# Gates of an mLSTM layer: column sums and the norm's spread inside blocks of products, and a new order of the row work on three engines

## The chip, the cores and the metric

The kernel runs on one core of a Trainium2 chip. Times are microseconds of device time for one execution. The core has TensorE (PE in the profile, with its weight loads as PEld), VectorE (DVE), ScalarE (ACT), GpSimd (POOL), and SyncE (SP), which here issues the DMAs. The number that counts is the median of several executions.

## The reference

One inference step of a decoder trunk with two layers. Layer 0 mixes tokens with a gated MLP, layer 1 with an mLSTM (a matrix memory with 8 heads); each layer is followed by a gated MLP with a causal convolution. There are 256 prompt tokens and a sample group of 8 sequences of 8 new tokens, 320 tokens in all, and the model width is 1024. All is fp32. The change lies at the start of the mLSTM layer. What is computed there, cut down:

```python
h = rmsnorm(x, g)                        # x * rsqrt(mean(x*x) + EPS) * g
p = h @ w_in                             # columns: q, k | v | o | i, f
qk, new_buf = causal_dwconv(p[..., :QK_B], conv_buf, conv_w, conv_b)   # 4 taps
qk = silu(qk)
ig = i_pre + b_i                         # 8 heads
lf = log_sigmoid(f_pre + b_f)
# per head, over the tokens (the prompt as one run, each sample sequence as one)
b = cumsum(lf)
m = max(b + m0, max over s <= t of (b_t - b_s + ig_s))        # running maximum
w_intra = exp(b_t - b_s + ig_s - m_t);  w_inter = exp(b_t + m0 - m_t)
g = exp(b_last - b + ig - m_last);      decay = exp(b_last + m0 - m_last)
```

So the gates need two running sums along the 320 tokens, one additive and one of maxima, in 8 rows (one for each head), and a handful of exponentials of them. `m` at the end of every sequence is an output.

## The kernel before, in words

**Layout.** Activations are kept transposed: features on the 128 partitions, the 320 tokens along the free axis. A product of an activation with a weight is done in *blocks*: one block makes 128 output features for all 320 tokens from the 1024 input features, in 8 steps `k` of 128.

**Three products for one.** To reach fp32 accuracy with a faster type, each operand is split into a high and a low half. For the activations these are `xh` and `xl`. A weight of a block arrives as `raw` (a DMA that SyncE issues, L152), ScalarE casts it to the high half `wh` (L179), and VectorE subtracts that from `raw` to make the low half `wl` (L180). A block is thus 24 products of 320 columns: for the mLSTM layer, `chunk` first does the 16 products that need `wh` (`xh` and `xl` for 8 steps) and then, in a second sweep, the 8 that need `wl`.

**Order.** The products and transposes of TensorE stay in the order of the program (`mm` and `tr` pin them). The other engines' instructions are put in order by a scheduler that has its own idea of when each will be ready; `tc.issue_after(x)` keeps what is made under it behind instruction x. Weights are ahead of their use: `take()` hands out the halves of the next block, issues the load of the fourth block ahead (L152), and issues the split of the next one (L179, L180). So a block's low half is made on VectorE during the block before it, and VectorE executes in its own fixed order: a low half that stands behind a waiting instruction comes late.

**The norm.** x is not normalised ahead of the products: the products are made of x times the norm's gain, and the factor for each token is multiplied into the results. `norm_cols` adds the squares over the features with three small products (`pc`, tokens on the partitions afterwards), VectorE scales the sums and adds EPS (`ms`, L294), ScalarE copies the sample group's 64 values to the other half of the partitions (L296), and GpSimd takes the power -1/2 (`rc`, L297). `norm_row(split=False)` turns these columns into a row that is the same on all partitions: three diagonal matrices `dg` made by VectorE (L307), one fp32 product of a matrix of ones with them (`pb`), and a copy by ScalarE (`rb`). Elsewhere in the kernel `norm_diag` and `norm_spread` do the same with the factors split into a high part (`rch`, `dg`) and a low part (`dgl`, made by ScalarE) and two products of the faster type.

**The gates** (`gates`, L716 to L810). First come 16 products `pg` for the gates' pre-activations, then the column sums (four small steps), then the blocks of head 0, in this order: q, first half of v, k, second half of v, first and second half of o. The text calls them the first to the sixth block. The spread `pb` stands between the first and the second. After the sixth, three transposes `pt` turn the finished rows `RS` into columns. The rows' work lies beside the blocks:

- `zi` is the pre-activation times `rb` plus the bias; ScalarE makes log-sigmoid from an Exp and a Ln (`az`, L760 and L761), with loads of its function tables (L759 is one) between functions of different tables, and a one-element Tanh (L762) brings the table that the convolutions need;
- VectorE scans (`b`), makes `a` and `aM`, scans for the maxima (`M`, L774), and then `m`, `wi` (two pieces, L781 and L782), the two pieces of `X`, and `g` (two pieces);
- ScalarE makes Exp of `wi`, `g` and `m`; the output `mo` and the rows `Xf` leave by DMA.

`qk_epi` (L812) is what follows a block of q or k: GpSimd copies three state columns in front of each sample sequence (`bpad<-bst`, L817), VectorE multiplies the block by `rb` into `bpad`, ScalarE starts the convolution (`bcv`, L824), VectorE adds three taps (L826), ScalarE takes a tanh (`bth`), VectorE makes `qs` by two products with it and the low half of q or k. `v_epi` only copies, on ScalarE. VectorE's order in this stage before is: q's epilogue as far as its inputs are there, the log-sigmoid rows, the scans, then k's taps and the low half of the sixth block.

The lines that the change touches:

## Time and profile before

| | us |
|---|---|
| median of 3 runs (lowest to highest) | 884.53 (884.48 to 884.72) |
| the profiled execution | 884.82 |
| its span in the profile | 883.1 |
| TensorE busy in it | 876.1 (99%) |
| VectorE busy | 672.4 (76%) |
| ScalarE busy | 514.3 (58%) |
| GpSimd busy | 109.5 (12%) |

The granted clock of TensorE in the profiled execution was 0.999 of the full one. The stage that the change touches runs from about 394 us to 418 us of the span.

How to read the rows that follow: a row of the timeline begins with the start and the time taken, in microseconds from the start of the span, then the engine, the line of the kernel, the operation, what it writes and reads by the program's names, its shape, and how many of the kind stand in a row (x3). A bracket at the end tells how long the engine was idle before and which instruction of another engine ended that. PE rows with several products give the time from the first one's start to the last one's end, and neighbouring rows overlap, because products are pipelined: the pace is read from start to start. A row of the chain that ended last has start, time taken, engine, tile and line.

### The profile page before, as it was taken

The page shows a single profiled execution, that of the slowest core. Times are in us where ns is not written, and L with a number is a line of the kernel's source. Part 1 is how long each engine was busy: PE and PEld are TensorE (multiplying, and loading weights), DVE is VectorE, ACT ScalarE, POOL GpSimd, SP SyncE. Part 2 cuts the span into 40 slices and gives each one's busy share as a digit, 9 for nine tenths or more (in the row PEclk, how much of TensorE's full clock was granted, in tenths as well). Part 3 has the DMA queues.
Part 4 walks back from the last instruction along what each step waited for, and adds up shares of the span by engine and source line. Part 5 has one row for each costly group of instructions (what it writes and reads, how often), then busy time and mean ns, then how long its engine had stood idle before and what let it go on. Part 6 is the DMA issues. An engine that isn't in the chain of part 4 may idle for free.

```text
span 883.1 us, 17016 instructions
## 1 busy us (share of the span) xinstructions
PE 876.1 (99%) x6421; PEld 859.1 (97%) x6421; DVE 672.4 (76%) x1288; ACT 514.3 (58%) x932; POOL 109.5 (12%) x287
## 2 busy tenths in 40 slices
PE   9999999999999999999999999999999999999997
PEld 7889999999999999999999999999999999999997
DVE  6866985678878865558999998878998788786443
ACT  6668553565555544447777776656766555554342
POOL 3200000020000000002433212203002000000000
PEclk9999999999999999999999999999999999999999
DMA  8653446644455455554747766665664444555551
GB/s 256 236 191 127 137 144 180 213 162 157 157 168 167 148 169 165 155 184 163 231 150 234 239 223 219 199 214 166 196 226 156 165 155 161 168 160 165 154 152 60
DMA packets 55238, 156.15 MB, mean 177 GB/s; under 512 B 7492, under 2 KB 13132, under 8 KB 55156
## 3 DMA queue, kind: packets, MB, share of 16 engines
q1 hardware_dynamic: 55156, 155.06, 55.4%
q8 instruction: 51, 0.84, 0.4%
q14 instruction: 31, 0.25, 0.1%
HBM read 143.05 MB, written 11.99 MB: 176 GB/s over the span
## 4 chain that ended last, share of the span: by engine, by line
PE 96%; DVE 2%; DMA 1%; ACT 0%; SPq 0%; issue 0%; POOL 0%; DVEq 0%
PE pm L75 83%; PE pv_a L75 6%; PE num L75 2%; PE pmix L75 1%; PE pcs L75 1%; PE psc L75 1%; PE pCp L75 1%; PE phn L78 1%; PE pv L78 1%; DMA raw<-in_a_wv 1%; PE pc L75 0%; PE pk L78 0%; DVE bcv L826 0%; DVE wl L180 0%; PE pg L75 0%; PE pb L75 0%
## 5 line engine op out<-in xcount | busy, mean ns | idle before, releaser
L180 DVE TENSOR_TENSOR wl<-raw,wh 128x1024 fp32r<-128x1024 f32 (+4 forms) x254 | 298.0, 1175 | 110.8 <-ACT wh L179 108.4
L179 ACT CAST wh<-raw 128x1024 fp32r<-128x1024 f32 (+4 forms) x254 | 255.5, 1006 | 209.0 <-PE pm L75 141.3
L75 PE MATMUL pm<-xh,wh 128*128 128x320 f32 x1216 | 356.6, 301 | 0.0
L75 PE MATMUL pm<-xl,wh 128*128 128x320 f32 x1216 | 354.5, 299 | 0.0
L75 PE MATMUL pm<-xh,wl 128*128 128x320 f32 x1216 | 308.9, 299 | 0.1
L75 PEld LDWEIGHTS pm<-xh,wh 128*128 128x128 f32 x1216 | 229.9, 189 | 0.3 <-ACT vTb L845 0.2
L75 PEld LDWEIGHTS pm<-xl,wh 128*128 128x128 f32 x1216 | 229.9, 189 | 0.2
L75 PEld LDWEIGHTS pm<-xh,wl 128*128 128x128 f32 x1216 | 211.9, 189 | 0.3 <-DVE wl L180 0.3
L75 PE MATMUL pm<-yh_f,wl 128*128 128x320 f32 x352 | 105.2, 299 | 0.0
L75 PE MATMUL pm<-yh_f,wh 128*128 128x320 f32 x352 | 105.2, 299 | 0.0
L75 PE MATMUL pm<-yl_f,wh 128*128 128x320 f32 x352 | 105.2, 299 | 0.0
L75 PEld LDWEIGHTS pm<-yh_f,wh 128*128 128x128 f32 x352 | 66.5, 189 | 0.0
L75 PEld LDWEIGHTS pm<-yl_f,wh 128*128 128x128 f32 x352 | 66.5, 189 | 0.0
L75 PEld LDWEIGHTS pm<-yh_f,wl 128*128 128x128 f32 x352 | 66.5, 189 | 0.0
L577 DVE SCALAR_TENSOR_TENSOR fcv<-fpad,vecs,fcv 128x336 f32<-128x336 f32 x88 | 49.5, 565 | 2.1 <-ACT fcv L575 0.7
L579 ACT ACTIVATE fgl<-fcv 128x256 f32<-128x256 f32 x44 | 18.3, 415 | 37.3 <-DVE fcv L577 37.3
L75 PE MATMUL pm<-yh_a,wl 128*128 128x320 f32 x128 | 38.4, 300 | 0.0
L75 PE MATMUL pm<-yh_a,wh 128*128 128x320 f32 x128 | 38.4, 300 | 0.0
L75 PE MATMUL pm<-yl_a,wh 128*128 128x320 f32 x128 | 38.3, 299 | 0.0
L75 PE MATMUL pm<-yhb,wh 128*128 128x320 f32 x128 | 35.9, 304 | 0.0
L75 PE MATMUL pm<-ylb,wh 128*128 128x320 f32 x128 | 35.5, 300 | 0.0
L345 DVE TENSOR_TENSOR xT<-pm,xT 128x320 f32<-128x320 f32 x39 | 18.9, 486 | 19.0 <-PE pm L75 19.0
(276 smaller groups left out, 1261.5 us busy)
## 6 DMA issues: line engine op xcount, KB each, us to landing
raw<-in_f_up SPq DMA_DIRECT2D x88, 512.0 KB, 3.3
raw<-in_b_win SPq DMA_DIRECT2D x48, 512.0 KB, 4.3
raw<-in_f_dn SPq DMA_DIRECT2D x32, 448.0 KB, 3.3
C<-in_C SPq DMA_DIRECT2D x32, 258.0 KB, 5.3
out_Cs<-C SPq DMA_DIRECT2D x32, 258.0 KB, 4.6
raw<-in_a_win SPq DMA_DIRECT2D x16, 512.0 KB, 3.3
raw<-in_a_wo SPq DMA_DIRECT2D x16, 512.0 KB, 5.2
raw<-in_f_dn SPq DMA_DIRECT2D x16, 512.0 KB, 3.5
```

The source lines that it names most:

```text
L75: self.pin(self.nc.tensor.matmul(out, lhsT, rhs, start=start, stop=stop, skip_group_check=skip))
L78: self.pin(self.nc.tensor.transpose(out, in_, ident))
L179: self.last_split = self.hold(nc.scalar.copy(wh[:, :kn, :], raw[:, :kn, :]))
L180: self.last_low = nc.vector.tensor_tensor(wl[:, :kn, :], raw[:, :kn, :], wh[:, :kn, :].bitcast(F32), op=SUB)
L345: self.nc.vector.tensor_tensor(x, ps[:, :T], x, op=ADD)
L577: nc.vector.scalar_tensor_tensor(cv, pd[:, i:i + NC], self.vec(w + i * KF), cv, op0=MULT, op1=ADD)
L579: nc.scalar.activation(gl[:, :TP], cv[:, :TP], AF.Gelu_apprx_tanh)
```

## The change

- `chunk` calls its hook `mid` only in the first sweep, so that a block with the low products last can have one. The column sums are called in the first block after two steps k (four products) and no longer ahead of it.
- The spread: the diagonals are made by `norm_diag(True)`, the high ones on VectorE, the low ones on GpSimd, and two products of the faster type take the place of the one fp32 product. They are called in the second block after two steps k.
- The second block is made (`p1`) ahead of the first block's epilogue in the program.
- GpSimd's copies of convolution state in `qk_epi` are issued after the last low diagonal, and so behind the power.
- A one-element Exp is issued right behind `rb`, and the first convolution step of q behind that; the Exp of the rows comes after this convolution step, and then Ln and the one-element Tanh, which q's tanh stands behind (`behind`). The copies of v's first half are issued after that Tanh.
- The scans and what belongs to them stand ahead of k's epilogue in the program.
- `m`, the two pieces of `wi` and the two pieces of `g` go from VectorE to GpSimd.
- The split that the fourth block's `take` issues (the fifth block's) is issued after the Ln, and what the sixth block's `take` issues after k's low half.

In the compiled program TensorE's instructions differ in the column sums and the spread alone. On SyncE's queue one load of `raw` moves behind the output of `mo` and the store of the rows.

```diff
+    def behind(self, ins, first):
+        self.tc.add_manual_dep(ins.ins, first.ins.name, mybir.DependencyInfo(
+            mybir.DependencyClass.NoSync, mybir.DependencyReason.DATA), reason="behind")
...
-                if mid and k == mid[0]:
+                if mid and k == mid[0] and sweep != 1:
                     mid[1]()
...
-    def norm_diag(self):
+    def norm_diag(self, pool=False):
...
         nc.vector.tensor_copy(rch, self.rc)
         nc.vector.tensor_tensor(rcl, self.rc, rcf, op=SUB)
...
             nc.vector.tensor_scalar(dh[:, c], self.ident[:, cs], rcf[:, t:t + 1], None, op0=MULT)
-            nc.scalar.activation(dl[:, c], self.ident[:, cs], AF.Copy, scale=rcl[:, t:t + 1])
+            if pool:
+                self.low_diag = nc.gpsimd.tensor_scalar(dl[:, c], self.ident[:, cs], rcl[:, t:t + 1], None, op0=MULT)
+            else:
+                nc.scalar.activation(dl[:, c], self.ident[:, cs], AF.Copy, scale=rcl[:, t:t + 1])
...
     def norm_spread(self, parts):
...
         self.mm(pb[:, :T], self.onesr, dh, True, False)
         self.mm(pb[:, :T], self.onesr, dl, False, True)
...
-                self.norm_cols(twice=True)
+                with tc.issue_after(self.acc_made.ins):
+                    p0 = self.block(KD, self.x_rhs, mid=(2, lambda: self.norm_cols(twice=True)))
                 with tc.issue_after(self.ms_made.ins):
                     nc.scalar.copy(sel, selr)
-                with tc.issue_after(self.acc_made.ins):
-                    p0 = self.block(KD, self.x_rhs)
-                self.norm_row(split=False)
+                rows = self.norm_diag(True)
+                with tc.issue_after(self.sq_made.ins):
+                    p1 = self.block(KD, self.x_rhs, mid=(2, lambda: self.norm_spread(rows)))
                 state_in(0)
                 nc.vector.tensor_tensor(zi, gr[:40], self.rb[:40, :], op=MULT)
-                qk_epi(0, 0, p0)
+                with tc.issue_after(self.rb_made.ins):
+                    first = nc.scalar.activation(mo[:, 0:1], bif[:8, 0:1], AF.Exp)
+                with tc.issue_after(first.ins):
+                    made = qk_epi(0, 0, p0)
                 nc.vector.tensor_scalar(zi, zi, bif[:, 0:1], None, op0=ADD)
                 nc.vector.scalar_tensor_tensor(az, z, -1.0, z, op0=MULT, op1=MAX)
-                nc.scalar.activation(az, az, AF.Exp, scale=-1.0)
+                with tc.issue_after(made[0].ins):
+                    nc.scalar.activation(az, az, AF.Exp, scale=-1.0)
                 ln = nc.scalar.activation(az, az, AF.Ln, bias=1.0)
                 with tc.issue_after(ln.ins):
-                    nc.scalar.activation(mo[:, 0:1], bif[:8, 0:1], AF.Tanh)
-                with tc.issue_after(self.sq_made.ins):
-                    ps = self.block(KD, self.x_rhs)
-                v_epi(0, 0, ps)
+                    first = nc.scalar.activation(mo[:, 0:1], bif[:8, 0:1], AF.Tanh)
+                self.behind(made[4], first)
+                with tc.issue_after(first.ins):
+                    v_epi(0, 0, p1)
                 state_in(0)
-                qk_epi(0, 1, self.block(KD, self.x_rhs))
                 nc.vector.scalar_tensor_tensor(z, z, 0.0, az, op0=ALU.min, op1=SUB)
...
                 nc.vector.tensor_tensor_scan(M, rst[:8, 1, :], aM, -1e30, op0=ADD, op1=MAX)
-                nc.vector.tensor_tensor(m, b, M, op=ADD)
+                low = qk_epi(0, 1, self.block(KD, self.x_rhs))[-1]
+                nc.gpsimd.tensor_tensor(m, b, M, op=ADD)
...
-                nc.vector.tensor_tensor(seg(wi[:, :64]), m0.unsqueeze(2).to_broadcast([8, NB, NS]), seg(M[:, TP:]), op=SUB)
-                nc.vector.tensor_tensor(wi[:, 64:72], m0, ML, op=SUB)
+                nc.gpsimd.tensor_tensor(seg(wi[:, :64]), m0.unsqueeze(2).to_broadcast([8, NB, NS]), seg(M[:, TP:]), op=SUB)
+                nc.gpsimd.tensor_tensor(wi[:, 64:72], m0, ML, op=SUB)
...
-                nc.vector.tensor_scalar(g[:, :TP], a[:, :TP], M[:, TP - 1:TP], None, op0=SUB)
-                nc.vector.tensor_tensor(seg(g[:, TP:]), seg(a[:, TP:]), ML.unsqueeze(2).to_broadcast([8, NB, NS]), op=SUB)
+                nc.gpsimd.tensor_scalar(g[:, :TP], a[:, :TP], M[:, TP - 1:TP], None, op0=SUB)
+                nc.gpsimd.tensor_tensor(seg(g[:, TP:]), seg(a[:, TP:]), ML.unsqueeze(2).to_broadcast([8, NB, NS]), op=SUB)
...
-                v_epi(0, 1, self.block(KD, self.x_rhs))
+                with tc.issue_after(ln.ins):
+                    ps = self.block(KD, self.x_rhs)
+                v_epi(0, 1, ps)
...
-                ps = self.block(KD, self.x_rhs)
+                with tc.issue_after(low.ins):
+                    ps = self.block(KD, self.x_rhs)
...
-                nc.gpsimd.tensor_copy(ps_[:, :, 0:3], stt[:, blk, :].rearrange("p (b e) -> p b e", e=3))
+                with tc.issue_after(self.low_diag.ins):
+                    nc.gpsimd.tensor_copy(ps_[:, :, 0:3], stt[:, blk, :].rearrange("p (b e) -> p b e", e=3))
...
-                nc.scalar.activation(cv, pd[:, 0:NC], AF.Identity, scale=self.vec(w), bias=self.vec(V_CB + blk))
+                made = [nc.scalar.activation(cv, pd[:, 0:NC], AF.Identity, scale=self.vec(w), bias=self.vec(V_CB + blk))]
...
+                return made + [self.parts[1]]
```

More of the change, by code (lines that the diff above doesn't have):

```diff
@@ L823, in qk_epi @@
                 w = V_CW + blk
-                nc.scalar.activation(cv, pd[:, 0:NC], AF.Identity, scale=self.vec(w), bias=self.vec(V_CB + blk))
+                made = [nc.scalar.activation(cv, pd[:, 0:NC], AF.Identity, scale=self.vec(w), bias=self.vec(V_CB + blk))]
                 for i in (1, 2, 3):
-                    nc.vector.scalar_tensor_tensor(cv, pd[:, i:i + NC], self.vec(w + 16 * i), cv, op0=MULT, op1=ADD)
+                    made.append(nc.vector.scalar_tensor_tensor(cv, pd[:, i:i + NC], self.vec(w + 16 * i), cv, op0=MULT, op1=ADD))
                 th = lp.tile([P, NC], F32, tag="th", name="bth", bufs=2)
-                nc.scalar.activation(th, cv, AF.Tanh, scale=0.5)
+                made.append(nc.scalar.activation(th, cv, AF.Tanh, scale=0.5))
                 qs = lp.tile([P, 384], F32, tag="qs", name="qs", bufs=2)
```

## Prediction

> **What bounds the kernel now.** I read the page first, then the chain that ended last around the change, then the timeline of each engine there.
>
> ```profile
> span 883.1 us, 17016 instructions
> PE 876.1 (99%) x6421; PEld 859.1 (97%) x6421; DVE 672.4 (76%) x1288; ACT 514.3 (58%) x932; POOL 109.5 (12%) x287
> ```
>
> TensorE is busy for 99% of the span. A change beside it can win only where TensorE waits, and it loses wherever its new order makes weights late. The profiled execution took 884.82 us around a span of 883.1; the median of the runs, 884.53, lies 0.29 lower. I take the sum as a difference and put it on the median.
>
> Two rows of the chain that ended last (start, us, what), and the timeline of TensorE:
>
> ```profile
> 414.28 1.15 DVE wl L180
> 415.48 1.35 PE pm L75 x8
> ```
> ```profile
> 394.50 0.34 PE L75 MATMUL pg<-xl,wl 128*128 128x320 f32 x1
> 394.84 0.83 PE L75 MATMUL pc<-ones,acc 128*128 128x2 f32 x6
> ...
> 395.75 0.30 PE L75 MATMUL pm<-xl,wh 128*128 128x320 f32 x1
> ...
> 399.41 0.81 PE L75 MATMUL pb<-dg,ones 128*128 128x320 f32 x2 [0.37 <-DVE dg L307]
> ...
> 400.19 0.30 PE L75 MATMUL pm<-xl,wh 128*128 128x320 f32 x1
> ...
> 403.31 0.30 PE L75 MATMUL pm<-xh,wh 128*128 128x320 f32 x1
> ...
> 409.83 0.30 PE L75 MATMUL pm<-xh,wh 128*128 128x320 f32 x1
> ...
> 415.13 0.30 PE L75 MATMUL pm<-xl,wh 128*128 128x320 f32 x1
> ...
> 416.67 0.49 PE L78 MATMUL pt<-ident,RS 128*128 128x128 f32 x3
> ```
>
> From 403.31 to 409.83 run two blocks, 48 products: one product costs 0.136 us, a block 3.26. At that pace the stage has three waits. The column sums could start at 394.64 and start at 394.84 (0.20). The first block's last product would end its slot at 395.75 + 23 x 0.136 = 398.87, and the spread starts at 399.41 (0.54). The eight low products of the sixth block could start at 415.27 and start at 415.48, when their low half is made (0.21, and some 0.1 behind the first of them). So at most about 1 us of waiting lies here, and a cheaper spread on top.
>
> ```profile
> 394.31 0.48 DVE L277 TENSOR_TENSOR acc<-acc,sq 128x320 f32<-128x320 f32 x1
> ...
> 396.31 1.21 DVE L180 TENSOR_TENSOR wl<-raw,wh 128x1024 fp32r<-128x1024 f32 x1
> 398.71 0.65 DVE L307 TENSOR_SCALAR dg<-ident,rc 128x128 f32<-128x128 f32 x3 [1.19 <-POOL rc L297]
> ...
> 406.29 0.43 DVE L830 SCALAR_TENSOR_TENSOR qs<-bth,bcv 128x256 f32<-128x256 f32 x1 [0.98 <-ACT bth L828]
> ...
> 408.07 0.48 DVE L768 SCALAR_TENSOR_TENSOR zi<-zi,az 8x320 f32<-8x320 f32 x1 [0.75 <-ACT az L760]
> ...
> 411.01 0.81 DVE L774 TENSOR_TENSOR_SCAN Xf<-rst,g 8x320 f32<-8x320 f32 x1
> ...
> 412.62 0.56 DVE L826 SCALAR_TENSOR_TENSOR bcv<-bpad,vecs,bcv 128x344 f32<-128x344 f32 x1
> ...
> 414.21 1.21 DVE L180 TENSOR_TENSOR wl<-raw,wh 128x1024 fp32r<-128x1024 f32 x1
> ```
> ```profile
> 396.77 1.10 POOL L817 COPY bpad<-bst 128x24 f32<-128x24 f32 x3 [3.16 <-DMA bst<-in_b_state]
> 397.83 0.84 POOL L297 TENSOR_TENSOR rc<-ms,mhalf 128x3 f32<-128x3 f32 x1
> ...
> 413.94 2.03 POOL L817 COPY bpad<-bst 128x24 f32<-128x24 f32 x1 [0.57 <-DVE wi L782]
> ```
>
> **Column sums in mid block.** They move four products back, to 395.18; `acc` is ready at 394.31 + 0.48 = 394.79, so the 0.20 goes. The sums keep their price, 394.84 to 395.75 less one product, 0.77.
>
> **Power ahead of the copies, and the spread.** GpSimd's power cannot simply start at 396.6, because GpSimd and VectorE block each other here. These rows show it:
>
> ```profile
> 30.50 1.22 DVE L180 TENSOR_TENSOR wl<-raw,wh 128x1024 fp32r<-128x1024 f32 x1
> ...
> 34.73 2.31 DVE L322 CAST rch<-rc 128x3 fp32r<-128x3 f32 x1
> ```
> ```profile
> 30.88 1.56 POOL L297 TENSOR_TENSOR rc<-ms,mhalf 128x3 f32<-128x3 f32 x1 [13.37 <-ACT ms L296]
> 34.64 2.37 POOL L406 TENSOR_TENSOR ws_a<-ws_a,trit 128x1024 f32<-128x1024 f32 x1 [2.20 <-DMA trit<-in_trit]
> ```
> ```profile
> 423.35 1.04 POOL L956 TENSOR_TENSOR kgz<-kgs,mk 128x512 fp32r<-128x512 f32 x1 [0.71 <-DVE kgs L933]
> ...
> 461.29 4.17 POOL L1008 TENSOR_TENSOR sl<-t,mhalf 128x3 f32<-128x3 f32 x1 [2.28 <-DVE t L1006]
> ```
>
> At 30.88 the power ends 0.72 after the low half beside it (31.72). So in the new order it ends 0.72 after the low half of 396.31, at 398.24 instead of 398.67. Then the spread's own form, from the rows where the kernel has it already:
>
> ```profile
> 181.49 0.17 DVE L322 CAST rch<-rc 128x3 fp32r<-128x3 f32 x1 [0.96 <-POOL rc L297]
> ...
> 181.77 0.64 DVE L326 TENSOR_SCALAR dg<-ident,rch 128x128 fp32r<-128x128 f32 x3
> ```
> ```profile
> 666.30 0.31 PE L75 MATMUL pb<-dg,onesr 128*128 128x320 f32 x1
> ...
> 666.60 0.30 PE L75 MATMUL pm<-xh,wh 128*128 128x320 f32 x1
> ```
>
> The high diagonals start 0.28 after the cast, at 398.56 (three in 0.64). The low ones now run on GpSimd, an operation the trace lacks; by 423.35 (1.04 for 512 columns) 128 columns cost 0.26, so 0.65 for the 320. Taking turns with VectorE for what they share they end near 399.9; if VectorE does not hold them at all, 399.3. TensorE gets there at 394.64 + 28 x 0.136 + 0.77 = 399.21, so it still waits some 0.55 and then pays 0.30 for two products where 399.41 to 400.19 less a product was 0.64. The third block starts at 402.78 instead of 403.31: **-0.53** (ends: -1.1 without the wait; +0.6 if the low half queued behind the high diagonals, 1.21, gets in ahead of the last low one).
>
> **Scans ahead of keys.** The row chain hangs on ScalarE:
>
> ```profile
> 401.75 0.67 ACT L824 ACTIVATE bcv<-bpad,vecs 128x344 f32<-128x344 f32 x1 [1.08 <-DVE bpad L819]
> 402.47 1.05 ACT L179 CAST wh<-raw 128x1024 fp32r<-128x1024 f32 x1
> 403.53 1.28 ACT L759 ACT_TABLE_LOAD   x1
> ...
> 407.57 0.47 ACT L760 ACTIVATE az<-az 8x320 f32<-8x320 f32 x1
> ...
> 409.78 0.20 ACT L762 ACTIVATE mo<-bif 8x1 f32<-8x1 f32 x1
> ```
>
> With `rb` copied by 400.73 come table load 1.28, Exp of one element 0.20, conv copy 0.67, Exp 0.47, load 1.28, Ln 0.47: 405.1, before 408.04. The last load, Tanh, and the two v copies fill ScalarE to 407.3, and only then comes the fifth block's high half (before at 402.47): 408.3, one microsecond ahead of that block at 409.3. On VectorE, from 408.07 to the second scan's end at 411.82 it took 3.75; now a tap replaces a split and the two q products (row 406.29) come in ahead of the copy, partly in an idle gap: 4.05. The scan ends near 409.2, 2.6 earlier.
>
> **Row steps on GpSimd, and what is queued behind them.** `m` (8x320) costs 0.65 by 423.35's rate; I take 0.7. It starts as the scan ends, and VectorE's split of q, two SBUF operands, stands behind it until 410.0. The fifth block's low half, made long before the change, now stands behind that split: 410.5 to 411.75. The block starts at 402.78 + 2 x 3.26 = 409.3 and wants it 16 products later, at 411.47: **+0.3**. The second small step (`wi`, 8 columns) waits behind this low half on GpSimd, to 411.9; then ScalarE's Exp, behind which k's conv copy (0.67) is queued, to 412.8; then VectorE's three taps (0.56 each), the two X pieces (8x392, by the row of 408.07 about 0.4 each) and the RS tail, some 2.4 to 2.6 with GpSimd's `g` steps between. The sixth block's low half thus runs from about 415.4 to 416.65. The block starts at 409.3 + 3.26 + 0.3 = 412.87 and wants it at 415.04: a wait of 1.6, where before were 0.3: **+1.3**. Behind it `khl` and X are in time at 417.8, which gives about 0.1 back.
>
> **Queues moved past.** SP: the outputs of `m` and the row store go out earlier, but one weight load that had a place ahead of them now waits for the row's Exp:
>
> ```profile
> 404.85 0.33 SPq L152 DMA_DIRECT2D raw<-in_b_win  x1
> ```
>
> It leaves near 413.5. Its cast comes at about 418 and its block after 429, so I cost it at nothing; if it landed 5 us later VectorE and ScalarE would still have 6. [...]
>
> **Sum.** -0.53 + 0.3 + 1.3 - 0.1 = about +1.0; the two late low halves may be half a microsecond off either way. 884.53 + 1.0 = 885.5; I say 885.6.
>
> **A rule weighed.** The rows at 34.64 and 34.73 show a cast of three elements held for the whole of a GpSimd multiply. [...] The row at 461.29 differs from taking turns: 4.17 for a power that alone costs 0.84, so more than two low halves went by. [...]
>
> **Rivals.** First, GpSimd starves (slower by far): a low half or a run of VectorE pieces gets in ahead of the last low diagonal or of `m` and `wi`. For it: 461.29, and 413.94 (2.03 for one copy; at 396.77 three take 1.10). Against: in the three copies of 396.77 GpSimd went as soon as the low half ended. It decides if the last low diagonal ends after 400.9: the spread +1.1, and the row chain, started later by as much, keeps both waits: 884.53 + 1.0 + 1.1 to 2.4, about 887.
>
> Second, faster than before: `wi`'s 8 columns get in ahead of the fifth block's low half. The margin is under 0.1 us (`wi` ends near 410.5, the low half asks at 410.5). Then Exp and k's conv copy come 1.1 earlier, the sixth low half ends about 415.5, its wait is 0.4 to 0.5 and the fifth's near 0.2: -0.53 + 0.2 + 0.15 - 0.1 = -0.3, 884.2; with a cheap `m` (0.55) -0.8, 883.7. It decides if the sixth low half ends before 415.3.
>
> Third, the gain is hidden and nothing is late: 884.5, inside the second.
>
> **Chances.** The forecast 0.45 (its own range 885.0 to 886.3), starving 0.27, `wi` in time 0.25, else 0.03. 0.2% is 1.8 us, about what a measurement can tell from no change. Faster by that needs under 882.76: all gains and no wait are -1.4, so 0.03. Slower, over 886.30: starving and the forecast's upper edge, 0.30. The rest, 0.67, is within. The range reaches to both rivals: 883.9 to 887.4.
>
> **What would show it.** `pc` at 395.2 and no wait before it; the power ending 0.7 after the low half; `pb`'s second product at 399.9 (401 if starved); the second scan ending near 409.2; the fifth and sixth blocks' low halves ending near 411.75 and 416.65, with TensorE's waits of 0.3 and 1.6 in front of their low products; `pt` at 417.8. Wrong if the sixth low half ends before 415.3, or if the spread's low part passes 401.

## The result and the profile after

The changed kernel takes 889.78 us (889.27 to 890.44, 6 runs) beside 884.50 for the kernel before on the same chip (884.24 to 884.72, 6 runs). The ratio is 1.006 [1.005, 1.007]: 5.3 us slower. The prediction said 885.6 with a range of 883.9 to 887.4; the time lies 2.4 us above that range, and above the 887 of the rival that was called starving.

```profile
span 888.1 us, 17011 instructions
PE 877.7 (99%) x6421; PEld 860.8 (97%) x6421; DVE 672.1 (76%) x1285; ACT 513.9 (58%) x933; POOL 118.4 (13%) x295
```

These are the page's first rows after the change. As many products run (6421), TensorE still shows 99%, and GpSimd (POOL) has 9 us more. Nothing in these rows tells of 5 us. The timeline of TensorE around the change does:

```profile
394.97 0.73 PE L80 MATMUL pc<-ones,acc 128*128 128x2 f32 x6
...
399.02 0.42 PE L80 MATMUL pb<-dg,onesr 128*128 128x320 f32 x1
...
401.04 0.42 PE L80 MATMUL pb<-dgl,onesr 128*128 128x320 f32 x1 [1.60 <-POOL dgl L333]
...
415.83 0.30 PE L80 MATMUL pm<-xl,wh 128*128 128x320 f32 x1
418.41 1.35 PE L80 MATMUL pm<-xh,wl 128*128 128x320 f32 x8 [2.28 <-DVE wl L185]
419.60 0.73 PE L83 MATMUL pt<-ident,RS 128*128 128x128 f32 x3
```

The column sums stand in mid block with no wait. The second product of the spread (`pb`) waits for GpSimd's low diagonals. The low products of the sixth block could start at 415.83 + 0.136 = 415.97 and start at 418.41: 2.44 us of waiting where the kernel before had 0.3. Behind that wait something else shows, in the windows of TensorE (window, its length, busy time and count, granted clock, DMA share, GB/s):

```profile
416.30:419.71 3.41, 1.30 (x9) 1.00 0.71 178
419.70:423.10 3.40, 3.33 (x16) 0.50 0.48 153
424.00:430.00 6.00, 6.00 (x47) 1.00 0.88 267
```

The first of these windows holds most of the wait. From 419.7 on, for 3.4 us, TensorE has half its clock. The column counts that time as busy (3.33 of 3.40), so it appears in no wait. The two engines that make the weights and the rows:

```profile
396.06 1.21 DVE L185 TENSOR_TENSOR wl<-raw,wh 128x1024 fp32r<-128x1024 f32 x1
...
398.89 1.21 DVE L185 TENSOR_TENSOR wl<-raw,wh 128x1024 fp32r<-128x1024 f32 x1
...
409.75 0.81 DVE L786 TENSOR_TENSOR_SCAN Xf<-rst,g 8x320 f32<-8x320 f32 x1
...
410.81 0.40 DVE L364 TENSOR_TENSOR qhl<-qs,qh 128x256 fp32r<-128x256 f32 x1
...
411.28 1.20 DVE L185 TENSOR_TENSOR wl<-raw,wh 128x1024 fp32r<-128x1024 f32 x1
...
417.04 0.18 DVE L808 COPY RS<-RS 64x64 f32<-64x64 f32 x1
417.15 1.21 DVE L185 TENSOR_TENSOR wl<-raw,wh 128x1024 fp32r<-128x1024 f32 x1
```
```profile
396.44 1.54 POOL L302 TENSOR_TENSOR rc<-ms,mhalf 128x3 f32<-128x3 f32 x1 [3.11 <-ACT ms L301]
398.48 2.51 POOL L333 TENSOR_SCALAR dgl<-ident,rcl 128x128 fp32r<-128x128 f32 x3 [0.50 <-DVE rcl L328]
...
410.65 2.55 POOL L788 TENSOR_TENSOR g<-g,Xf 8x320 f32<-8x320 f32 x1 [2.40 <-DVE Xf L786]
413.17 0.29 POOL L794 TENSOR_TENSOR wi<-bif,Xf 8x64 f32<-8x64 f32 x1
...
413.61 0.92 POOL L803 TENSOR_SCALAR g<-RS,Xf 8x256 f32<-8x256 f32 x1
415.20 0.89 POOL L804 TENSOR_TENSOR g<-RS,Xf 8x64 f32<-8x64 f32 x1
```

The row of 410.65 is the step called `m` (its buffer is named `g` there). It stands at GpSimd for 2.55 us. It starts before VectorE's split of q (410.81) and before the fifth block's low half (411.28), and it ends 0.72 after the latter. The three low diagonals take 2.51, around the low half of 398.89.

To see where the 5 us are, the starts of the same products in the two traces were subtracted, and the offset that the two executions had ahead of the gates (-0.24) was taken off. By 440 us the changed kernel is 5.20 later:

| Place | Predicted, us | Measured, us |
|---|---|---|
| column sums | -0.20 | -0.28 |
| spread, with the column sums | -0.53 | +0.94 |
| fifth block's low half | +0.3 | 0 |
| sixth block's low half (wait 0.3 to 2.44) | +1.3 | +2.2 |
| half clock, 3.4 us | not in the sum | +1.7 |
| after it, to 440 us | -0.1 | +0.34 |

### The profile page after: what moved, and what is told of

The parts are those of the page before. It is cut to its first block, busy times and chain, and to the rows that moved or that the text cites. A ratio compares the mean times of both kernels' runs of the same rounds, so it can differ in the third digit from the quotient of the medians.

```text
span 888.1 us, 17011 instructions
## 1 busy us (share of the span) xinstructions
PE 877.7 (99%) x6421; PEld 860.8 (97%) x6421; DVE 672.1 (76%) x1285; ACT 513.9 (58%) x933; POOL 118.4 (13%) x295
## 4 chain that ended last, share of the span: by engine, by line
PE 94%; DVE 2%; ACT 1%; POOL 1%; DMA 1%; issue 1%; SPq 0%; ACTq 0%; DVEq 0%
PE pm L80 80%; PE pv_a L80 6%; PE num L80 2%; PE pmix L80 1%; PE psc L80 1%; PE pcs L80 1%; DMA Mb<-rows 1%; PE phn L83 1%; PE pCp L80 1%; PE pv L83 1%; DVE bcv L843 0%; PE pw L80 0%; ACT wh L184 0%; PE pc L80 0%; DVE wl L185 0%
```

## The experiments

None of these kernels leaves out a part of the computation. Medians, with the ratio to the kernel before on the same chip (884.3 to 884.5):

| Kernel | us | ratio [95%] | later by 440 us |
|---|---|---|---|
| after | 889.78 | 1.006 [1.005, 1.007] | +5.20 |
| e1: low diagonals on ScalarE | 888.77 | 1.0048 [1.0031, 1.0065] | +3.59 |
| e2: VectorE's split held behind them | 888.59 | 1.0048 [1.0033, 1.0063] | +4.66 |
| e3: `m` alone | 889.13 | 1.0058 [1.0043, 1.0073] | +4.83 |
| e4: norm part alone | 884.35 | 0.9999 [0.9990, 1.0008] | -0.01 |
| e5: e1, k's conv copy first | 887.92 | 1.0040 [1.0026, 1.0054] | +3.87 |
| e6: e5, `g` on VectorE | 886.10 | 1.0019 [1.0010, 1.0028] | +1.76 |
| e7: no row step on GpSimd | 884.77 | 1.0006 [0.9997, 1.0016] | +0.19 |
| e8: the new order alone | 885.49 | 1.0014 [1.0004, 1.0023] | +1.54 |
| e9: e7, two queues mended | 883.23 | 0.9988 [0.9979, 0.9997] | -0.82 |

The last column comes from a single execution of each kernel, with its offset ahead of the gates taken off (e1's execution was 1.1 us late there, e2's 0.9 early), so it follows the medians only to within 0.8 us.

### e1: the low diagonals on ScalarE

```diff
-                rows = self.norm_diag(True)
+                rows = self.norm_diag()
...
-                with tc.issue_after(self.low_diag.ins):
+                with tc.issue_after(self.rc_made.ins):
                     nc.gpsimd.tensor_copy(ps_[:, :, 0:3], ...)
```

> The changed kernel with one edit: ScalarE makes the three low diagonals, GpSimd no longer does (the conv-state copies are issued after the power). Theory A, VectorE's low half of 398.89 starves GpSimd's low diagonals: they now follow ScalarE's cast (ends 398.56) in 0.93, so the spread's second product starts at 399.5 to 399.6 in place of 401.04. Everything behind it moves up by 1.5 and the sixth block still waits about 2.4 for its low half: 888.3 (887.9 to 888.7). Theory B, the price lies in the spread's place inside the second block or in its two products: 889.8 as before this edit. Theory C, the row chain alone sets the end, and it is not tied to the spread: 889.8 as well, with the sixth block's wait grown to about 3.9.

Measured: 888.77, just above theory A's range and 1.0 us less than the changed kernel. ScalarE's and GpSimd's timelines, then TensorE's, then its window:

```profile
399.89 0.94 ACT L335 ACTIVATE dgl<-ident,rcl 128x128 fp32r<-128x128 f32 x3
```
```profile
410.49 2.56 POOL L788 TENSOR_TENSOR g<-g,Xf 8x320 f32<-8x320 f32 x1 [2.40 <-DVE Xf L786]
```
```profile
418.25 2.34 PE L80 MATMUL pm<-xh,wl 128*128 128x320 f32 x8 [2.29 <-DVE wl L185]
```
```profile
418.25:421.60 3.35, 3.35 (x14) 0.53 0.67 231
```

The three diagonals take 0.94 on ScalarE instead of 2.51, and the spread no longer waits for them. But `m` keeps its 2.56, the sixth block its wait (2.29) and TensorE its 3.4 us at half clock. So the spread is about 1 to 1.6 us of the loss, and the larger part does not hang on it: TensorE and the row chain both came earlier by about that much, and the wait between them stayed.

### e2: VectorE's split held behind the low diagonals

```diff
+                touch = nc.vector.tensor_copy(rp.tile([P, 1], F32, name="touch"), rows[1][:, T - 1:T].bitcast(F32))
...
-                low = qk_epi(0, 1, self.block(KD, self.x_rhs))[-1]
+                with tc.issue_after(touch.ins):
+                    p2 = self.block(KD, self.x_rhs)
+                low = qk_epi(0, 1, p2)[-1]
```

The copy of one column reads the last low diagonal, so the low half that took a turn between them now waits.

> The changed kernel with a VectorE copy of one element that reads the last low diagonal, and the weight split that started at 398.89 (the fourth block's) behind it; GpSimd still makes the low diagonals. [...] Theory D, GpSimd itself needs 0.7 to 1.4 for such a piece: the second product stays at 401.0, the split moves to 401.1 to 402.3, the rows are late by 0.4 and the time is 890.2.

Measured: 888.59. GpSimd, VectorE and TensorE:

```profile
397.79 1.70 POOL L333 TENSOR_SCALAR dgl<-ident,rcl 128x128 fp32r<-128x128 f32 x3 [0.50 <-DVE rcl L328]
```
```profile
399.52 0.15 DVE L761 COPY touch<-dgl 128x1 f32<-128x1 f32 x1 [1.25 <-POOL dgl L333]
```
```profile
399.54 0.41 PE L80 MATMUL pb<-dgl,onesr 128*128 128x320 f32 x1 [0.79 <-POOL dgl L333]
```

With VectorE idle for 1.25 us beside them the three still take 1.70 (0.70, 0.60 and 0.44 for the 64 columns of the last). So of the 2.51, 1.70 is the price of the operation itself and 0.8 is the low half that got in. The prediction had 0.65, from a two-operand multiply of 512 columns in 1.04. Most of the miss in this term is a wrong price, not starving. The time lies below the 890.2 of theory D, and the sixth block's wait (2.33 us of idling) and the half clock behind it (417.63 to 421.04) are still there.

### e3: `m` alone

```diff
                 nc.gpsimd.tensor_tensor(m, b, M, op=ADD)
+                touch = nc.vector.tensor_copy(rp.tile([8, 1], F32, name="touch"), m[:, T - 1:T])
+                self.behind(made[-1], touch)
...
-                with tc.issue_after(ln.ins):
+                with tc.issue_after(ln.ins), tc.issue_after(touch.ins):
                     ps = self.block(KD, self.x_rhs)
```

q's split and the fifth low half are held until `m` is done.

> The changed kernel with a VectorE copy of one element that reads m, and VectorE's low half of q and the fifth block's low half behind it; the scheduler also puts k's first conv step ahead of the Exp of wi. Theory A: m, which took 2.55 while VectorE passed it three times, takes 0.7 to 1.1 (the k block's multiply by rb runs beside its start); the fifth low half ends at about 413.2 in place of 412.48 and is waited for by some 0.5, the taps start by 413.3 in place of 414.6, the sixth low half is waited for by about 1 in place of 2.45, and the k epilogue no longer holds the scores: 888.1 (887.6 to 888.7). Theory D (GpSimd itself needs over 2 for 8x320): m still takes 2.5, everything behind it on VectorE is late by 1.5 to 2, 890.5 to 891.5.

Measured: 889.13, between the ranges of the two theories and only 0.65 below the changed kernel. GpSimd and TensorE:

```profile
410.37 0.86 POOL L788 TENSOR_TENSOR g<-g,Xf 8x320 f32<-8x320 f32 x1 [2.40 <-DVE Xf L786]
```
```profile
417.25 1.35 PE L80 MATMUL pm<-xh,wl 128*128 128x320 f32 x8 [0.76 <-DVE wl L185]
...
419.63 0.39 PE L80 MATMUL psc<-qh,kh 128*128 128x256 f32 x1 [0.70 <-ACT kh L364]
...
430.49 0.46 PE L80 MATMUL num<-vh,Ps 128*128 128x258 f32 x2 [1.01 <-DVE vh L926]
```

Alone, `m` takes 0.86; so 1.7 of its 2.55 is VectorE going by. The sixth block's wait falls to 0.9, with a new one of 0.5 at the fifth, and the half clock is gone (here k's conv copy also went ahead of the Exp of `wi`, at 410.82, so the shorter wait is not the work of `m` alone). Yet the end moves little: against the kernel before, new delays of 0.9, 1.1 and 0.5 us stand behind, the last at 439.88, where TensorE waits for a copy of v. One is k's split, late because the row chain's Exps and casts fill ScalarE; another is head 1's first product with its rows, late because the load of those rows is. The gain was given back to the next late things in line.

### e4: the norm part alone

```diff
-                self.norm_cols(twice=True)
+                with tc.issue_after(self.acc_made.ins):
+                    p0 = self.block(KD, self.x_rhs, mid=(2, lambda: self.norm_cols(twice=True)))
...
-                self.norm_row(split=False)
+                rows = self.norm_diag()
+                with tc.issue_after(self.sq_made.ins):
+                    p1 = self.block(KD, self.x_rhs, mid=(2, lambda: self.norm_spread(rows)))
```

This is the kernel before with the column sums and the spread in mid block, the power ahead of the conv-state copies, and the low diagonals on ScalarE. The order of the gates' rows stays as it was.

> The kernel before with the norm's part alone: column sums in the first block after two steps, the spread by two products in the second block after two steps with the low diagonals on ScalarE, and the power ahead of the conv-state copies; the rows' order and engines as before. Theory A: the spread waits some 0.4 and the third block starts about 0.55 earlier than before, the row chain starts earlier too and the wait of 0.3 at the sixth block stays or goes: 883.9 (883.6 to 884.1). Theory B (the spread's place in the block costs 0.9): 885.4. If the row chain of before is what holds the sixth block, whenever the spread ends, the gain is lost there: 884.5.

Measured: 884.35, ratio 0.9999 [0.9990, 1.0008]. TensorE:

```profile
398.83 0.41 PE L75 MATMUL pb<-dg,onesr 128*128 128x320 f32 x1
...
414.83 1.35 PE L75 MATMUL pm<-xh,wl 128*128 128x320 f32 x8 [0.44 <-DVE wl L180]
```

The spread's first product runs without a wait, its second follows as directly, and products behind it are 0.58 earlier than before (0.27 by the sums, 0.31 by the spread). At the sixth block's low half that is gone: its wait is 0.6 instead of 0.3 (the row's 0.44 of idling and the part of a product before it), and the rest follows by 440 us. The low half's time is set by the row chain and not by TensorE, so an earlier TensorE only waits longer there. So with the low diagonals on ScalarE a gain of the size predicted for the spread (-0.53) was there, and it was worth nothing at the end.

### e5: k's conv copy ahead of the row Exps

```diff
-                low = qk_epi(0, 1, self.block(KD, self.x_rhs))[-1]
+                kmade = qk_epi(0, 1, self.block(KD, self.x_rhs))
+                low = kmade[-1]
...
-                nc.scalar.activation(Xf[:, T:392], wi, AF.Exp)
+                with tc.issue_after(kmade[0].ins):
+                    decay = nc.scalar.activation(Xf[:, T:392], wi, AF.Exp)
...
+                with tc.issue_after(decay.ins):
                     nc.scalar.activation(RS[32:40, 0:T], g, AF.Exp)
```

Beside e1, k's conv copy on ScalarE no longer stands behind the Exp that waits for `wi`.

> As the kernel with the low diagonals on ScalarE, and ScalarE does k's first conv step ahead of the Exp of wi (the Exps of g and m stay behind that Exp). In that kernel the sixth low half ran from 416.98, waited for 2.45, and TensorE's granted clock was 0.50 for 3.4 us behind it. Theory T1, k's conv step queued behind wi's Exp sets the sixth low half: the taps start at about 412.4 in place of 414.44, the sixth low half ends 1.5 earlier, the wait falls to about 0.9, no slow clock follows, and the time falls by 3 to 885.3 to 885.8. Theory T2, g on GpSimd sets it: the copy inside RS stands ahead of the sixth low half on VectorE and waits for ScalarE's Exps, these for g's second piece, which GpSimd finished at 415.94: the wait stays at 2.2 to 2.5 with the slow clock behind it, 888.2 to 888.8.

Measured: 887.92, just below theory T2's range. GpSimd, VectorE, TensorE and TensorE's window behind the wait:

```profile
409.05 3.04 POOL L789 TENSOR_TENSOR g<-g,Xf 8x320 f32<-8x320 f32 x1 [2.40 <-DVE Xf L786]
```
```profile
415.12 0.22 DVE L811 COPY RS<-RS 64x64 f32<-64x64 f32 x1 [0.16 <-ACT RS L808]
```
```profile
416.52 1.35 PE L80 MATMUL pm<-xh,wl 128*128 128x320 f32 x8 [2.00 <-DVE wl L185]
```
```profile
416.50:420.00 3.50, 2.78 (x19) 1.00 0.82 274
```

The taps come earlier, but the wait is still 2.2 us (2.00 idle): the sixth low half now stands behind the small copy of `RS`, which waits for ScalarE's Exps, which wait for the second piece of `g` on GpSimd. After the change this second path is close behind the first: ScalarE's Exp of `g` ends at 416.60, the last tap at 417.13. And `m` took 3.04: four VectorE instructions that started after it (from 409.21 to 410.81) ended before it, a tap among them. What went is the half clock: after 2.00 us of idling it stayed at 1.00, where 2.28 and 2.29 had brought 0.50. Why is taken up in e10.

### e6: `g` back on VectorE as well

```diff
-                nc.gpsimd.tensor_scalar(g[:, :TP], a[:, :TP], M[:, TP - 1:TP], None, op0=SUB)
-                nc.gpsimd.tensor_tensor(seg(g[:, TP:]), ...)
+                nc.vector.tensor_scalar(g[:, :TP], a[:, :TP], M[:, TP - 1:TP], None, op0=SUB)
+                nc.vector.tensor_tensor(seg(g[:, TP:]), ...)
```

> As the run above, and g's two pieces back on VectorE, where they stand ahead of the fifth block's low half; m and wi stay on GpSimd. Theory T2: the copy inside RS no longer waits; the fifth low half is 0.55 later and waited for by about 0.4, m is starved until that low half ends (412.9) and wi follows at 414.0, the taps and X's pieces end at 416.4, the sixth low half ends near 417.8 and is waited for by about 1.5; no slow clock: 886.0 (885.5 to 886.5). Theory T3, any wait of 1.3 or more brings the slow clock: 1.7 more, 887.7. Theory T1: no change against the run above.

Measured: 886.10. GpSimd and VectorE:

```profile
408.98 0.85 POOL L789 TENSOR_TENSOR g<-g,Xf 8x320 f32<-8x320 f32 x1 [2.40 <-DVE Xf L786]
```
```profile
409.14 0.97 DVE L364 TENSOR_TENSOR qhl<-qs,qh 128x256 fp32r<-128x256 f32 x1
```

TensorE waits 0.79 at the fifth block and 0.78 at the sixth, where e5 waited 2.2 at the sixth alone. So GpSimd's two pieces of `g` did hold that low half. The time is as theory T2 had it, but not by its steps: it had `m` starved, with waits of 0.4 and 1.5. Here `m` took 0.85 and was not passed; VectorE's split of q, which started 0.16 after it, took 0.97 instead of 0.40. (The small second step of `wi` was then held, for 2.09.) After the change the split also started 0.16 after `m`, and there it passed.

### e7: no row step on GpSimd

```diff
+                with tc.issue_after(ln.ins):
+                    p4 = self.block(KD, self.x_rhs)
+                with tc.issue_after(self.last_low.ins):
+                    nc.vector.tensor_tensor(m, b, M, op=ADD)
-                nc.gpsimd.tensor_tensor(m, b, M, op=ADD)
...
+                nc.vector.tensor_tensor(wi[:, 64:72], m0, ML, op=SUB)
-                nc.gpsimd.tensor_tensor(wi[:, 64:72], m0, ML, op=SUB)
...
+                nc.vector.tensor_scalar(g[:, :TP], a[:, :TP], M[:, TP - 1:TP], None, op0=SUB)
-                nc.gpsimd.tensor_scalar(g[:, :TP], a[:, :TP], M[:, TP - 1:TP], None, op0=SUB)
```

Beside e1, with the conv copy where e1 has it, `m`, both steps of `wi` and both of `g` are on VectorE, and the fifth block's low half is put ahead of `m`.

> The changed kernel with the low diagonals on ScalarE and m, wi and g on VectorE, behind the fifth block's low half; the rest of the new order (scans ahead of k's epilogue, the fifth split behind the Ln, one-element Exp and Tanh) is kept. Theory G, GpSimd's part of the change costs it: the taps run from 412.4 with m, wi and g between them, the sixth low half ends at about 416.5 and is waited for by 0.7, no slow clock, 884.8 (884.3 to 885.3). Theory O, the order costs it, because the fifth low half and the taps now stand in the row stage: the sixth low half still waits 2 or more and the slow clock follows, 887.5 to 888.5.

Measured: 884.77, 5.0 us below the changed kernel and level with the kernel before. VectorE and TensorE:

```profile
413.43 1.21 DVE L185 TENSOR_TENSOR wl<-raw,wh 128x1024 fp32r<-128x1024 f32 x1
```
```profile
414.69 1.35 PE L80 MATMUL pm<-xh,wl 128*128 128x320 f32 x8
```

The sixth low half ends 3.7 us earlier than after the change and no wait is left in front of its products. Apart from the place of the fifth low half all else of the change is still in, so what was moved to GpSimd, the diagonals and the row steps together, makes nearly the whole of the loss; what that place is worth by itself was not run.

### e8: the new order alone

```diff
-                    p0 = self.block(KD, self.x_rhs, mid=(2, lambda: self.norm_cols(twice=True)))
+                    p0 = self.block(KD, self.x_rhs)
...
-                    p1 = self.block(KD, self.x_rhs, mid=(2, lambda: self.norm_spread(rows)))
+                    p1 = self.block(KD, self.x_rhs)
...
-                nc.gpsimd.tensor_tensor(m, b, M, op=ADD)
+                nc.vector.tensor_tensor(m, b, M, op=ADD)
```

Column sums and spread as before the change, all row steps on VectorE; the scans stay ahead of the keys.

> The norm as in the kernel before (column sums ahead of the first block, one fp32 product), all row steps on VectorE, and the changed kernel's order of the scans, the one-element Exp and Tanh, the fifth split behind the Ln and the copies of conv state behind the power. Theory G: about as the kernel before, 884.5 (884.2 to 885.0). Theory O: g and m and X's pieces stand with the taps ahead of the sixth low half, which ends near 416.8 and is waited for by 1.5, and RS is late by 0.4: 886.1 (885.6 to 886.8), and 887.5 or more if the slow clock follows.

Measured: 885.49, ratio 1.0014 [1.0004, 1.0023]. TensorE:

```profile
414.90 1.35 PE L80 MATMUL pm<-xh,wl 128*128 128x320 f32 x8 [0.70 <-DVE wl L185]
...
426.92 0.46 PE L80 MATMUL num<-vh,Ps 128*128 128x258 f32 x2 [0.84 <-DVE vh L925]
```

The order by itself costs about 1.1 us, just below what was expected of it: the sixth block's wait, and then head 1's first product. e7, which has the norm part and also the fifth low half ahead of `m`, is 0.7 below e8; which of the two earns that was not separated. The norm part alone earned nothing in the old order (e4).

### e9: two queues mended

```diff
-                o_epi(0, 0, self.block(KD, self.x_rhs))
+                p5 = self.block(KD, self.x_rhs)
                 with tc.issue_after(low.ins):
+                    o_epi(0, 0, p5)
+                mb = lp.tile([P, 392], F32, name="Mb1")
+                first = nc.sync.dma_start(mb, I["rows"][1:2, :].to_broadcast([P, 392]))
+                S[1]["rows"] = mb
+                with tc.issue_after(low.ins), tc.issue_after(first.ins):
                     ps = self.block(KD, self.x_rhs)
```

Beside e7, k's last split goes ahead of the first output gate's steps, and head 1's rows are loaded ahead of a block's weights instead of at the head's start.

> The kernel without GpSimd's rows (low diagonals on ScalarE; m, wi and g on VectorE behind the fifth low half) with two moves: VectorE's multiply for the first half of o is issued after the low half of k, and the load of head 1's row stands right behind the store of the rows on SyncE's queue, ahead of the weight loads. That kernel's trace stood 0.59 ahead of the kernel before after the spread and gave back 0.42 waiting for k's low half and 0.43 at 434.9, behind ScalarE, which waits for head 1's row. If these two waits are what is left of the order's price, both go: 883.8 (883.5 to 884.1), faster than the kernel before by some 0.6. If VectorE or ScalarE is simply full in this stage, the waits come back elsewhere: 884.4 to 884.8.

Measured: 883.23 (11 runs) against 884.26 (15 runs) for the kernel before, ratio 0.9988 [0.9979, 0.9997]: 1.0 us faster than before and 6.5 faster than the changed kernel, and 0.3 below the range that was expected. Both waits of e7 (0.24 at 416.85, 0.38 at 435.59) are gone from TensorE's timeline. The issue of that load on SP's queue in e9 and in the changed kernel:

```profile
414.54 0.34 SPq L819 DMA_DIRECT2D Mb<-rows  x1
```
```profile
423.45 0.37 SPq L868 DMA_DIRECT2D Mb<-rows  x1
```

In the changed kernel it goes out at 423.45 with weight loads in front of it, in e7 at 419.56. After the change it lands 5.57 later by the chain, and ScalarE waits 2.64 for it:

```profile
429.13 0.51 ACT L885 ACTIVATE w<-Mb,cols 128x256 f32<-128x256 f32 x1 [2.64 <-DMA Mb<-rows]
```

The two moves were run together, and which of them earns how much of the 1.5 us between e7 and e9 stays open.

### e10: waits of many sizes ahead of TensorE

```diff
                 gate(b + 1, self.block(KD, self.x_rhs))
+                if l and i:
+                    n = (4, 5, 6, 7, 8, 5, 6, 7, 8, 9)[i - 1]
+                    scr = lp.tile([P, 512], F32, tag="scr", name="scr", bufs=1)
+                    nc.gpsimd.tensor_copy(scr[:, 0:1], yh[:, b, 0:1].bitcast(F32))
+                    for _ in range(n):
+                        nc.gpsimd.memset(scr, 1.0)
+                    pz = self.psa.tile([P, 512], F32, tag="pa", name="pz")
+                    self.mm(pz[:, :2], scr[:, :P], self.ones[:, :2], True, True)
```

In the feed-forward part of the kernel before, a small product behind a run of n GpSimd fills makes TensorE wait ten times, for 1.9 to 4.7 us. It adds work and leaves none out.

> The kernel before, with ten waits put into the second conv MLP, 13 us apart: TensorE waits there for a small product whose operand GpSimd fills by 4, 5, 6, 7, 8, 5, 6, 7, 8 and 9 writes of 512 columns, behind a copy of what the block before made. The waits should come out between about 1 and 4.5 us. Theory H: a wait of TensorE of about 2.3 us or more is followed by about 3.4 us at a granted clock of 0.50, and one under about 2.2 by none; each such stretch costs 1.7 us on top of the wait. Theory I: the slow clock in the gates' stage had another cause (the mix of small products there): the clock stays at 1.00 behind every wait in the middle of plain blocks. Theory J: only waits of more than 3.4 us bring it.

Measured: 946.98 (one run), as the waits are in the time. TensorE's timeline at four of them, then its windows around the first three:

```profile
686.60 0.38 PE L75 MATMUL pz<-ones,scr 128*128 128x2 f32 x2 [1.92 <-POOL scr L611]
...
702.62 0.38 PE L75 MATMUL pz<-ones,scr 128*128 128x2 f32 x2 [2.49 <-POOL scr L611]
...
720.90 0.59 PE L75 MATMUL pz<-ones,scr 128*128 128x2 f32 x2 [3.08 <-POOL scr L611]
...
861.88 0.59 PE L75 MATMUL pz<-ones,scr 128*128 128x2 f32 x2 [4.69 <-POOL scr L611]
```
```profile
682.93:686.35 3.42, 1.75 (x13) 1.00 0.56 212
686.35:689.76 3.41, 3.17 (x23) 1.00 0.50 180
700.00:703.41 3.41, 0.92 (x7) 1.00 0.46 160
703.42:706.82 3.40, 3.40 (x15) 0.50 0.41 148
717.07:720.48 3.41, 0.76 (x6) 1.00 0.42 154
720.49:727.30 6.81, 6.39 (x24) 0.50 0.24 77
```

After 1.92 us of idling the clock stays at 1.00. After each of the other nine waits (2.49 to 4.69) it is 0.50, for 3.41 us twice and for 6.83 seven times. A product starts every 0.267 us there instead of 0.136. So the half clock follows from a wait alone, in a stage that has nothing to do with the gates, and neither the data nor the row steps are needed for it: theory I and theory J are out. Theory H had the stretch too short for most of these waits.

When the clock changes tells more. The nine stretches begin at 703.41, 720.48, 740.96, 761.44, 781.92, 798.99, 819.47, 839.95 and 860.42. The distances are 17.07 and 20.48 us, five and six times 3.413, and the stretches last one or two times as much. So in these traces the clock changes only at fixed points of time, 3.41 us apart, that don't follow the waits. The windows above are cut at these points, counted on in steps of 3.413 where the clock didn't change. The wait of 2.49 lies in one interval between two points (3.41 less 0.92 busy), and the next interval has half clock. The wait of 1.92 is cut by a point: 1.67 us of idling fall into one interval, 0.25 into the next, and the clock stays. Where the wait still ran at the point (0.26 to 1.45 us of it in the interval at half clock), a second interval at half clock followed.

The gates' rows agree. After the change 2.12 us of the 2.28 lie in the interval from 416.30 to 419.71, and the clock halves at 419.71; in e1 (2.29) and e2 (2.33) the whole wait lies in one interval. In e5 a point at 415.91 (counted back from the change of clock at 883.54, at the end of its trace) cuts the wait of 2.00 into 1.39 and 0.61. Counted by interval, the clock stayed with 1.67 us of idling or less, and halved with 2.12 or more; counted by the whole wait, the two sides are 2.00 and 2.28. These runs don't separate the two counts. If the interval counts, e5 was spared by where its wait happened to fall.

## Why the prediction was wrong

The prediction had +1.0 and the trace by 440 us has +5.2. The miss of 4.2 is the half clock (1.7, a term that was not in the sum), the spread (1.47, the price of GpSimd's low diagonals), the sixth block's wait (0.9), less the fifth block's wait that did not come (0.3), and 0.4 behind. By its own steps:

- **Column sums.** Right: they moved, the wait went, -0.28 for -0.20.
- **Power.** Right: it took 1.54 and ends 0.71 after the low half beside it (396.06 + 1.21 to 396.44 + 1.54), as the row at 30.88 had said 0.72; at 397.83 in the kernel before it took 0.84.
- **Low diagonals on GpSimd: the first step that failed.** "128 columns cost 0.26, so 0.65 for the 320" took the nearest row, a two-operand multiply of 512 columns, for a multiply by one scalar per partition in three narrow pieces. Undisturbed they take 1.70 (e2). From 398.56 to 399.9 the prediction gave them 1.34, a turn with VectorE in it; they took 2.51, and 1.05 of these 1.17 is the price. Of the term's miss of 1.47 (-0.53 to +0.94) the diagonals' later end (400.99 for 399.9) is 1.1, and 0.24 more is that this execution ran that much ahead of the kernel before when it came to them. The term's own ends (-1.1 and +0.6) did not hold it.
- **Second scan near 409.2.** It ended at 410.56, later by the 1.4 to 1.5 us by which the spread was late, so the chain behind the spread was counted rightly.
- **`m`, and its order with VectorE.** Its price was near (0.7; 0.86 alone in e3, 0.85 in e6). But "VectorE's split of q ... stands behind it" was the wrong way round: `m` came first, and three VectorE instructions that started after it (410.81, 411.14, 411.28) ended before it (2.55 in all), in e5 four (3.04). The fifth block's +0.3 fell away for the same reason. In e6 the split of q, started 0.16 after `m`, was held (0.97 instead of 0.40). So no run shows that the split has to stand behind `m`: of two that started 0.16 after it, one passed and one was held. In the sum the wrong order is small, because `wi` was put behind the fifth low half in any case: from the scan's end to the end of `wi` the prediction had 2.7 (409.2 to 411.9) and the trace has 3.1 (410.56 to 413.62). From there to the end of the sixth low half the prediction had 4.75 and the trace has 4.7: that long chain was right, and started late.
- **Wait of 1.6 at the sixth block.** 2.44: the right wait, in the right place, too small. The low half came 1.7 later than predicted (418.36 for 416.65), by the spread and by `m`; TensorE came only 0.9 later (415.97 for 415.04), because the fifth block's wait was missing. In e5 the mechanism behind it shows further: with `wi`'s part taken away the low half is still held, by `g` on GpSimd through ScalarE's Exps and the `RS` copy, which the prediction passed over with "GpSimd's `g` steps between".
- **Half clock.** Not in the prediction at all, nor in a rival: 1.7 us, half of 3.41. No idling of 1.67 us or less brought it in these traces, so at the forecast's wait of 1.6 leaving it out would have been right; at the measured one it was not.
- **Queues moved past.** The weight load that moved brought no wait of TensorE for its own block, as costed. But it does not move alone: between the store of the rows and the load of head 1's row, SyncE's queue has two weight loads before the change (415.45 to 419.37) and four after it (416.05 to 423.34), so head 1's row leaves at 423.45 instead of 419.54. The prediction did not look at what runs out next: head 1's rows, and k's split. After the change the 0.34 is at a late copy of v (440.56), which the chain traces back to that row; whenever an experiment mended something ahead of them (e3, e5), they took the gain: some 2.5 us there.

The rival called starving is the one whose condition was met, at its very edge: "if the last low diagonal ends after 400.9", and it ended at 400.99. Its mechanism, VectorE's pieces getting in ahead of the last low diagonal and of `m`, is what the trace shows. That its condition was met is partly luck: it took the low half that got in (0.8) and the diagonals' own price, which the rival did not have; by an estimate from their start at 398.48 either alone would have ended them by 400.2. Its price (887) lacks the half clock's 1.7. The rival that ended faster, `wi` in time, was never near: `wi` ended 3 us after its point of decision.

That GpSimd's steps are the loss is shown by e7, which keeps the rest of the change but for the fifth low half's place: 5.0 of 5.3 us. e8, which has no row step or diagonal on GpSimd either, but the fifth low half where the changed kernel has it and the norm as before the change, is 4.3 below the changed kernel. How the 5.0 divides can be read from the ladder after, e1, e5, e6, e7: 1.0 for the diagonals, 0.85 for the half clock and the conv copy's place, 1.8 for `g`, 1.3 for `m` and `wi` (with the fifth low half's new place, and the conv copy back where e1 has it). These shares are argued, not shown one by one: another order of the steps would give others, since each wait hides the next.

## What to carry to other kernels

Here a step handed to GpSimd beside busy VectorE cost its own price plus the VectorE instructions that passed it (`m`: 0.86 alone, 2.55 and 3.04 passed), or it held VectorE instead (e6: the split of q took 0.97 instead of 0.40), so put one there only where the chain behind it has that slack; price it from a row with the same form and width, not from the number of elements (the low diagonals: 1.70 in e2, 0.65 by the columns of another form). Where TensorE is the bound, a late weight can be paid twice, as after the change: 2.44 us of waiting, then 3.4 us at a granted clock of 0.50, which no wait and no busy share shows, so look at the granted clock in windows behind each long wait. And before a gain is counted, look up what is late next: here an earlier spread by itself was worth nothing (e4), while the same edits with the new order of the rows and two queues mended behind them won 1.0 us (e9).

## What was not expected of the hardware

A short wait was enough for half the clock: 2.12 us of idling in an interval of 3.41 (after the change) brought 3.41 us at a granted clock of 0.50, and most longer waits 6.83; from full clock, 1.67 and less in an interval brought none. The intervals stand still while the waits move, so the half clock begins inside a long wait (e10) or behind its end: 0.2 us behind in e1, 0.7 in e2, 1.3 after the change.

A GpSimd operation beside VectorE does not always go first: `m` was passed by three VectorE instructions that started after it (2.55), and by four in e5 (3.04), while in e6 it took 0.85 and VectorE's split waited (0.97 instead of 0.40), and in the three conv-state copies quoted in the prediction (1.10 from 396.77) GpSimd went as soon as the low half beside them (396.31 + 1.21) ended: they were done 0.35 later. What decides between the two was not settled.
